# MLP up-projection of a hybrid decoder layer: product 2 of two tile pairs computed together by a second seven-product scheme

## The chip, the core and the metric

The kernel runs on one core of one Trainium2 chip. TensorE (PE) multiplies matrices, VectorE (DVE), ScalarE (ACT) and GpSimd (POOL) work elementwise, SyncE (SP) and the queues of ACT and POOL issue DMA transfers. Each engine takes its instructions in the order in which they were built; semaphores tie the engines together. The metric is the device time of one execution in microseconds.

## The reference

One layer of a decoder, fp32, for 1024 prompt tokens and 8 x 8 decode tokens: RMS norm, one input projection, two mixers (retention and sliding-window attention), output projection, residual; then the part that matters here:

```python
h = x + jnp.concatenate([o_r, o_s], axis=-1) @ w_out
hf = rms_norm(h, norm_ffn_gain)
h = h + jnp.square(jax.nn.relu(hf @ w_up)) @ w_down     # w_up (1024, 4096), w_down (4096, 1024)
```

All 1088 tokens (T) go through the layer as one batch.

## The kernel before

**Three passes for one product.** Every fp32 operand is split into a high part (a cast to the multiplier's type on ACT) and a low part (the difference, on DVE): `halve`, lines 792 and 793. `mm3` multiplies high by high, low by high and high by low into one PSUM bank (lines 176 to 178), so a 128x128 block times 272 columns is three matmuls.

**Seven products.** The up stage works on tile pairs `fp` = 0 to 15, 256 features each (two tiles of 128 rows). The 1024 inputs are two halves of 512, the 1088 tokens are two superchunks `s` of two quarters of Q = 272. So for each pair and superchunk there is a 2x2 by 2x2 block product, and it is made of seven products in place of eight (Strassen's scheme in Winograd's form): `PROD = (1, 2, 6, 5, 7, 4, 3)`. The right sides (`ops`: B11, B21, B22 and T1 to T4, split) are made once and stay in SBUF. The left sides come from `left`: a generator that loads the pair's four blocks a11, a12, a21, a22 as two raw tiles of 512 KB (`rawload`, issued on ACT's queue, line 807, three buffers with the tag "raw"), makes four sums on POOL (`comb`, line 1047: numbers 5, 6, 7 and 3) and splits each of the seven for PE (`wsplit`, tags wa and wb, four buffers each). A product of one superchunk is 4 x 3 = 12 matmuls.

**Results.** Banks x, y and z for each superchunk collect the products: 1, 6, 7 and 4 add up in x, and ACT copies x after 1, 6 and 7 (line 1142) because the running value is needed; before PE writes x again, that copy must be done. Product 2 goes into bank y, which DVE adds to the copy of product 1 (line 1121). DVE then scales (`act`, line 1126), ACT squares into `ra` (line 1127), POOL makes the four differences for the down stage's own seven products (`sub`, line 1175: four for each superchunk), and SP stores both to DRAM (`u_d`). `ra` and `rb` have one buffer, so ACT's squares of the next pair wait until POOL has read those of this one.

**The order.** The order of the products is written out in `up`; where the instructions of the engines land relative to each other is decided by the tile scheduler, which keeps each engine's queue as one fixed list. `issue_after` ties an instruction behind another. In the stretch of pairs 3 to 8 and on, `split_down` prepares pieces of w_down ahead (lines 1211 to 1216).

Of the kernel before, what the change touches and what calls it, by code (L numbers as in the profile page):

```python
# [36 lines left out]
def hymba_layer(ctx: ExitStack, tc: tile.TileContext, a: dict, o: dict):  # L37
# [753 lines left out]
    def halve(hi, lo, src, lo_eng):  # L791
        nc.scalar.copy(hi, src)  # L792
        lo_eng.tensor_tensor(lo, src, hi.bitcast(F32), ALU.subtract)  # L793
# [243 lines left out]
    def left(order, src, name, lo_eng, raw_tag="raw", raw_pool=None, s_tag="S", s_pool=None, tags=("wa", "wb"), raws=None, sums=None, stored=None):  # L1037

        r1, r2 = raws or (
            rawload(src[:, i * 1024 : i * 1024 + 1024], f"{name}_r{i + 1}", raw_tag, raw_pool) for i in range(2)  # L1040
        )
        a11, a12, a21, a22 = r1[:, :512], r1[:, 512:], r2[:, :512], r2[:, 512:]
        have = {1: a11, 2: a12, 4: a22, **(sums or {})}

        def comb(i, p_, q_, op):
            t_ = have[i] = (s_pool or mid).tile([P, 512], F32, tag=s_tag, name=f"{name}_s{i}", bufs=10 if s_tag == "Sb" else 4)
            nc.gpsimd.tensor_tensor(t_, p_, q_, op)
# [52 lines left out]
    um = ux.enter_context(pool("u", side="right"))  # L1100

    last_sub, last_store, last_sq = {}, [None], [None]

    def up(fp):
        gen = chain(ready, gen0) if fp == 0 else left(
            PROD, a["w_up"][fp], f"wu{fp}", nc.vector, tags=("wa", "wa", "wb", "wb"))
        x, y, z = ([bank(f"ps{n}{s}") for s in range(2)] for n in "xyz")
        home = {1: (x, True), 2: (y, True), 6: (x, False), 5: (z, True), 7: (x, False), 4: (x, False), 3: (z, False)}
        ra, rb = ([um.tile([P, n, Q], F32, tag=f"r{n}{s}", name=f"r{n}t{fp}_{s}") for s in range(2)] for n in (3, 4))
        held, wait, ws = {}, [], {}  # L1110
        order = [(i, s) for i in PROD for s in range(2)]
        if fp == 0:

            order = [(1, 0), (1, 1), (2, 0), (6, 0), (5, 0)] + [(i, 1) for i in (2, 6, 5)] + order[8:]

        def tq(n, s):
            return um.tile([P, Q], F32, tag="tq", name=f"{n}{fp}_{s}", bufs=9)

        def add(n, s, bank_):
            t_ = held[n, s]  # L1120
            nc.vector.tensor_tensor(t_, t_, bank_, ALU.add)
            return t_

        def act(t_, src, s, h, dst):

            nc.vector.scalar_tensor_tensor(t_, src, 0.0, rsf[:, s, h, :], ALU.max, ALU.mult)  # L1126
            return nc.scalar.activation(dst, t_, AF.Square)

        for i, s in order:
            if i not in ws:  # L1130
# [9 lines left out]
            if i in (1, 6, 7):  # L1140
                t_ = held[i, s] = tq(f"m{i}", s)
                nc.scalar.copy(t_, bk)  # L1142
# [22 lines left out]
            if i == 3:
                t_ = add(6, s, bk)
                if fp == 15 and s:
                    with tc.issue_after(squared.ins):
# [4 lines left out]
                t1, t2, t3, t4 = (rb[s][:, i_, :] for i_ in range(4))
                eng = nc.vector if fp in (0, 15) and s else nc.gpsimd
                sub = lambda o_, p_, q_: eng.tensor_tensor(o_, p_, q_, ALU.subtract)
# [32 lines left out]
    def split_down(f, c):  # L1208
# [222 lines left out]
```

## Time and profile before

| what | value |
|---|---|
| median of 3 runs | 1182.31 us (1181.42 to 1185.21) |
| profiled execution | 1183.0 us, span 1181.2 us |
| PE, DVE, ACT, POOL busy | 99%, 70%, 43%, 42% of the span |
| up stage, first to last psx matmul of op_0h | 496.0 to 835.1 us |
| granted clock | 0.999 |
| HBM read, written | 117.45 MB, 55.71 MB |

In a row of groups stand the line, the engine, the operation, output and inputs, shapes, count, busy time and mean of one in ns, and the idle time before them with what ended it. In a row of waits stand who waited for whom, the total, the count and the longest. In a row of windows stand the stretch, its length, and for PE, weight load, DVE, ACT and POOL the busy time with its count, then granted clock, DMA share and GB/s. In a row of the timeline stand start, duration, engine and instruction. Transfers have their size and the median time from issue to landing.

### The profile page before, as it was taken

The page shows a single profiled execution, that of the slowest core. Times are in us where ns is not written, and L with a number is a line of the kernel's source. Part 1 is how long each engine was busy: PE and PEld are TensorE (multiplying, and loading weights), DVE is VectorE, ACT ScalarE, POOL GpSimd, SP SyncE. Part 2 cuts the span into 40 slices and gives each one's busy share as a digit, 9 for nine tenths or more (in the row PEclk, how much of TensorE's full clock was granted, in tenths as well). Part 3 has the DMA queues.
Part 4 walks back from the last instruction along what each step waited for, and adds up shares of the span by engine and source line. Part 5 has one row for each costly group of instructions (what it writes and reads, how often), then busy time and mean ns, then how long its engine had stood idle before and what let it go on. Part 6 is the DMA issues. An engine that isn't in the chain of part 4 may idle for free.

```text
span 1181.2 us, 23556 instructions
## 1 busy us (share of the span) xinstructions
PE 1168.7 (99%) x9405; PEld 1124.5 (95%) x9405; DVE 831.6 (70%) x1551; ACT 512.5 (43%) x1060; POOL 492.7 (42%) x393
## 2 busy tenths in 40 slices
PE   8999999999999999999999999999999999999998
PEld 8999988989879899999999999999999999999998
DVE  7556868732258769888666667667678787888676
ACT  8343544553234447654444444444643423333231
POOL 0135334332255542457666766667374142053000
PEclk9999999999999999999999999999999999999999
DMA  7221334333625554343454445534795446443225
GB/s 248 73 62 63 96 104 163 104 118 90 192 67 175 180 169 160 126 136 143 149 176 141 166 157 171 170 123 151 235 383 179 149 163 203 150 157 98 77 59 189
DMA packets 106181, 174.69 MB, mean 148 GB/s; under 512 B 12319, under 2 KB 71647, under 8 KB 105815
## 3 DMA queue, kind: packets, MB, share of 16 engines
q1 hardware_dynamic: 92711, 129.04, 33.0%
q10 hardware_dynamic: 10800, 35.23, 9.2%
q0 software_dynamic: 2560, 8.91, 2.4%
q8 instruction: 74, 1.21, 0.4%
q14 instruction: 36, 0.29, 0.1%
HBM read 117.45 MB, written 55.71 MB: 147 GB/s over the span
## 4 chain that ended last, share of the span: by engine, by line
PE 83%; DVE 6%; DMA 5%; issue 3%; POOL 1%; ACT 1%; SPq 0%; DVEq 0%; POOLq 0%; ACTq 0%
PE psd L177 9%; PE psd L178 9%; PE psd L176 9%; PE psx L176 5%; PE psx L178 5%; PE psx L177 5%; PE psz L176 2%; PE psz L178 2%; PE psz L177 2%; PE pst L176 2%; PE pst L177 2%; PE pst L178 2%; PE psf L176 2%; PE psf L178 2%; PE psf L177 2%
## 5 line engine op out<-in xcount | busy, mean ns | idle before, releaser
L177 PE MATMUL psd<-uh,wd_w 128*128 128x272 f32 x896 | 259.2, 289 | 0.0
L178 PE MATMUL psd<-ul,wd_w 128*128 128x272 f32 x896 | 257.6, 288 | 0.3 <-DVE ul L793 0.3
L176 PE MATMUL psd<-uh,wd_w 128*128 128x272 f32 x896 | 257.8, 288 | 0.0
L176 PEld LDWEIGHTS psd<-uh,wd_w 128*128 128x128 f32 x896 | 169.1, 189 | 0.0
L178 PEld LDWEIGHTS psd<-ul,wd_w 128*128 128x128 f32 x896 | 168.5, 188 | 0.5 <-DVE ul L793 0.5
L177 PEld LDWEIGHTS psd<-uh,wd_w 128*128 128x128 f32 x896 | 168.4, 188 | 0.0
L1299 DVE TENSOR_TENSOR a<-a,psd 128x272 f32<-128x272 f32 x248 | 101.5, 430 | 50.7 <-PE psd L178 50.6
L793 DVE TENSOR_TENSOR wu_w<-wu_s,wu_w 128x512 fp32r<-128x512 f32 x64 | 58.4, 917 | 54.1 <-ACT wu_w L792 53.3
L792 ACT CAST wd_w<-wd_s 128x512 fp32r<-128x512 f32 x64 | 36.8, 617 | 113.2 <-PE psd L178 100.4
L793 DVE TENSOR_TENSOR ul<-ur,uh 128x1088 fp32r<-128x1088 f32 (+1 forms) x57 | 81.9, 1465 | 5.5 <-ACT uh L792 5.5
L176 PE MATMUL psx<-op_1h,wu_w 128*128 128x272 f32 x256 | 74.2, 290 | 0.3 <-ACT m L1142 0.3
L176 PE MATMUL psx<-op_0h,wu_w 128*128 128x272 f32 x256 | 74.1, 290 | 0.0
L178 PE MATMUL psx<-op_1l,wu_w 128*128 128x272 f32 x256 | 74.1, 289 | 0.0
L178 PE MATMUL psx<-op_0l,wu_w 128*128 128x272 f32 x256 | 74.1, 289 | 0.0
L177 PE MATMUL psx<-op_1h,wu_w 128*128 128x272 f32 x256 | 73.7, 288 | 0.0
L177 PE MATMUL psx<-op_0h,wu_w 128*128 128x272 f32 x256 | 73.7, 288 | 0.0
L1126 DVE SCALAR_TENSOR_TENSOR m<-m,rsf 128x272 f32<-128x272 f32 x96 | 71.3, 743 | 2.9 <-ACT rsf L915 0.5
L792 ACT CAST uh<-ur 128x1088 fp32r<-128x1088 f32 (+1 forms) x57 | 59.8, 1085 | 16.7 <-PE psd L177 9.1
L366 POOL TENSOR_TENSOR sp<-sp,ssp 128x1024 f32<-128x1024 f32 (+1 forms) x16 | 28.6, 1789 | 88.4 <-DVE ssp L365 60.0
L176 PE MATMUL psf<-hnh,wqk_hi 128*128 128x384 f32 (+1 forms) x192 | 63.5, 331 | 0.2 <-DVE qkst L518 0.2
L178 PE MATMUL psf<-hnl,wqk_hi 128*128 128x384 f32 (+1 forms) x192 | 63.1, 329 | 0.0
L177 PE MATMUL psf<-hnh,wqk_lo 128*128 128x384 f32 (+1 forms) x192 | 62.8, 327 | 0.0
(345 smaller groups left out, 3619.2 us busy)
## 6 DMA issues: line engine op xcount, KB each, us to landing
ur<-u_d SPq DMA_DIRECT2D x53, 544.0 KB, 5.0
u_d<-r4t SPq DMA_DIRECT2D x32, 544.0 KB, 3.2
wu_r<-in_w_up ACTq DMA_DIRECT2D x32, 512.0 KB, 4.5
wd_r<-in_w_down ACTq DMA_DIRECT2D x30, 512.0 KB, 6.8
u_d<-r3t SPq DMA_DIRECT2D x32, 408.0 KB, 2.7
y<-in_xY POOLq DMA_DIRECT2D x16, 272.0 KB, 3.5
y_d<-y POOLq DMA_DIRECT2D x16, 272.0 KB, 3.1
yt<-y_d SPq DMA_DIRECT2D x16, 272.0 KB, 2.8
```

The lines of the kernel that those rows point to most:

```text
L176: nc.tensor.matmul(ps, lh, rh, start=first, stop=False, skip_group_check=more)
L177: nc.tensor.matmul(ps, ll, rh, start=False, stop=False, skip_group_check=more)
L178: return nc.tensor.matmul(ps, lh, rl, start=False, stop=last, skip_group_check=more)
L366: nc.gpsimd.tensor_tensor(s, s, ss.unsqueeze(2).broadcast_to([P, 4, n]), ALU.mult)
L792: nc.scalar.copy(hi, src)
L793: lo_eng.tensor_tensor(lo, src, hi.bitcast(F32), ALU.subtract)
L1126: nc.vector.scalar_tensor_tensor(t_, src, 0.0, rsf[:, s, h, :], ALU.max, ALU.mult)
L1299: added[i] = nc.vector.tensor_tensor(to, to, ps, ALU.add).ins
```

## The change

For pairs 4 to 15 product 2, which is a12 times B21, leaves the pair. The product 2 of pairs `fp` and `fp + 1` over both superchunks is seen as one 2x2 by 2x2 product itself: two pairs by two quarters of 256 inputs on the left, two quarters by two superchunks on the right. It is made of seven small products of 2 x 3 = 6 matmuls each (`second`), run between the products of the pair ahead (`trail`: odd pairs 3 to 13), into banks ps2x, ps2y and ps2z. ACT copies four of the small results (line 1192) and DVE adds three (line 1195) into the tiles `tp2`; in its own pair, product 1 is then added to `tp2` (line 1253), scaled in place (1254) and squared (1266). Pairs 0 to 3 stay as they were. The right sides of the small products, three of them split sums of quarters of B21, are made once in pairs 2 and 3 (`prepare`). The left sides come from `left2`: one more raw load of 512 KB for two pairs (a12 of both, line 1153), four sums of 128x256 on POOL (1160 to 1167), three splits of 512 and one of 256. Of the `tq` buffers six are left of nine. Lines of the changed kernel move: copies of products are line 1257, comb stays 1047, differences are 1296, the sums with banks are 1229, scaling and squares 1234 and 1235.

```diff
@@ in left: comb
-            nc.gpsimd.tensor_tensor(t_, p_, q_, op)
+            last_comb[name, i] = nc.gpsimd.tensor_tensor(t_, p_, q_, op).ins
@@ new, ahead of up
+    L2 = 4
+    quarter = {(kh, s): [t_[:, 2 * kh : 2 * kh + 2, :] for t_ in ops[B21][s]] for kh in range(2) for s in range(2)}
+    tcomb = {i: [l2.tile([P, 2, Q], F32R, tag=f"x{i}{x}", name=f"x{i}{x}") for x in "hl"] for i in (2, 3, 4)}
+    tcomb[1] = quarter[0, 1]
+    RIGHT2 = {1: quarter[0, 0], 2: quarter[1, 0], 3: quarter[1, 1], 4: tcomb[4], 5: tcomb[1], 6: tcomb[2], 7: tcomb[3]}
...
+    def prepare():
...
+        for k in range(2):
...
+            e22 = join(nc.vector, last_stt[0], quarter[1, 1], k)
+            e21 = join(nc.gpsimd, behind, quarter[1, 0], k)
+            e11 = join(nc.gpsimd, behind, quarter[0, 0], k)
+            e12 = join(nc.vector, last_stt[0], quarter[0, 1], k, home)
+            nc.vector.tensor_tensor(e22, e22, e12, ALU.subtract)
+            nc.vector.tensor_tensor(e12, e12, e11, ALU.subtract)
+            nc.vector.tensor_tensor(e11, e22, e11, ALU.add)
+            nc.vector.tensor_tensor(e21, e21, e11, ALU.subtract)
...
+    def left2(fp, tags):
+        raw = mw.tile([P, 1024], F32, tag="raw", name=f"wp{fp}_r", bufs=3)
+        nc.scalar.dma_start(
+            raw.rearrange("p (f n) -> p f n", f=2), a["w_up"][fp : fp + 2, :, 512:1024].rearrange("f p n -> p f n")
+        )
+        a11, a12, a21, a22 = (raw[:, 256 * i : 256 * i + 256] for i in range(4))
+        yield wsplit(raw[:, :512], tags[0], f"wp{fp}_a", nc.vector)
...
+        nc.gpsimd.tensor_tensor(s1, a21, a22, ALU.add)
+        nc.gpsimd.tensor_tensor(s2, s1, a11, ALU.subtract)
+        nc.gpsimd.tensor_tensor(s3, a11, a21, ALU.subtract)
+        yield wsplit(s23, tags[1], f"wp{fp}_s23", nc.vector)
+        w = (mid if tags[2] == "wb" else mw).tile([P, 2, 512], F32R, tag=tags[2], name=f"wp{fp}_d", bufs=4)
+        halve(w[:, 0, :256], w[:, 1, :256], a22, nc.vector)
+        yield w
+        nc.gpsimd.tensor_tensor(s4, a12, s2, ALU.subtract)
+        yield wsplit(s14, tags[3], f"wp{fp}_s14", nc.vector)
+    def second(fp, tags):
...
+        copies = {1: (0, 0), 6: (0, 1), 7: (1, 1), 4: (1, 0)}
+        sums = {2: (0, 0), 5: (1, 1), 3: (0, 1)}
...
+            for k in range(2):
+                lh, ll = (got[n][:, j, c0 + k * 128 : c0 + k * 128 + 128] for j in range(2))
+                rh, rl = (v[:, k, :] for v in RIGHT2[i])
+                mm3(bk, lh, ll, rh, rl, first and k == 0, k == 1, not first)
...
@@ in up
+        trail = fp >= L2 - 1 and fp % 2 == 1 and fp < 15
+        prods = PROD if fp < L2 else (1, 6, 5, 7, 4, 3) if fp == 15 else (1, 5, 6, 7, 4, 3)
...
-        order = [(i, s) for i in PROD for s in range(2)]
+        order = [(i, s) for i in prods for s in range(2)]
+        if trail:
+            n = len(prods) - 5
+            for at, i in ((n, 1), (n, 2), (n + 1, 6), (n + 2, 7), (n + 3, 4), (n + 4, 5), (n + 5, 3)):
+                order.insert(2 * at + len(order) - 2 * len(prods), (i, 2))
...
+            if i == 1 and fp >= L2:
+                t_ = tp2[fp, s]
+                nc.vector.tensor_tensor(t_, t_, bk, ALU.add)
+                last_stt[0] = nc.vector.scalar_tensor_tensor(t_, t_, 0.0, rsf[:, s, 0, :], ALU.max, ALU.mult).ins
...
+            if fp >= L2 and (i, s) == (6 if trail else 7, 1):
+                for s_ in range(2):
+                    with tc.issue_after(last_copy[0]):
+                        nc.scalar.activation(ra[s_][:, B11, :], tp2[fp, s_], AF.Square)
```

Two places of the built order, on the engines that wait there. The first is POOL, from the sums for one pair to the differences of the pair before. In names, the number behind wu is the pair, s5, s6, s7 and s3 are comb's sums, wp10 belongs to the small products of pairs 10 and 11, r4t7 holds the differences of pair 7. Before:

```order
L1047 TENSOR_TENSOR wu9_s5_8355<-wu9_r2_8289 128x512
L1047 TENSOR_TENSOR wu9_s6_8357<-wu9_s5_8355,wu9_r1_8287 128x512
L1047 TENSOR_TENSOR wu9_s7_8417<-wu9_r1_8287,wu9_r2_8289 128x512
L1047 TENSOR_TENSOR wu9_s3_8491<-wu9_r1_8287,wu9_s6_8357 128x512
L1175 TENSOR_TENSOR r4t7_0_7753<-r127_0_7977,r3t7_0_7751 128x272
L1175 TENSOR_TENSOR r4t7_0_7753<-r3t7_0_7751,r127_0_7977 128x272
```

and now, behind wu9_s5, wu9_s6 and the first two sums of wp10 (one row each):

```order
L1161 TENSOR_TENSOR wp10_s2_8485<-wp10_s1_8486,wp10_r_8432 128x256
L1296 TENSOR_TENSOR r4t7_0_7853<-r127_0_8115,r3t7_0_7851 128x272
L1296 TENSOR_TENSOR r4t7_0_7853<-r3t7_0_7851,r127_0_8115 128x272
L1167 TENSOR_TENSOR wp10_s1_8486<-wp10_r_8432,wp10_s2_8485 128x256
L1296 TENSOR_TENSOR r4t7_0_7853<-r3t7_0_7851,r4t7_0_7853 128x272
L1296 TENSOR_TENSOR r4t7_1_7854<-r127_1_8136,r3t7_1_7852 128x272
L1296 TENSOR_TENSOR r4t7_1_7854<-r3t7_1_7852,r127_1_8136 128x272
L1296 TENSOR_TENSOR r4t7_0_7853<-r3t7_0_7851,r4t7_0_7853 128x272
L1047 TENSOR_TENSOR wu9_s7_8542<-wu9_r1_8397,wu9_r2_8399 128x512
L1296 TENSOR_TENSOR r4t7_1_7854<-r3t7_1_7852,r4t7_1_7854 128x272
L1047 TENSOR_TENSOR wu9_s3_8639<-wu9_r1_8397,wu9_s6_8456 128x512
```

The four sums of a pair stood together ahead of the eight differences; now the last two, which are the last readers of the raw tiles, stand behind the sums of wp10 and seven differences.

The second place is ACT at the same time: the copies of product 7 (m7 and the pair, m78 for pair 8) and what stands ahead of them. Before:

```order
L1127 ACTIVATE r3t7_0_7751<-m17_0_7774 128x272 [waits DMAHW1_49,DVE_49,Pool_49]
L1142 COPY m67_0_7842<-psx0_7745 128x272 [waits PE_49]
L807 DMA wu9_r2_8289<-in_w_up 128x1024 [waits DMAHW6_49,DVE_49]
L1127 ACTIVATE r3t7_1_7752<-m17_1_7788 128x272 [waits DMAHW2_49,Pool_49]
L1142 COPY m67_1_7856<-psx1_7746 128x272 [waits PE_49]
L792 CAST wu8_w5_8124<-wu8_s5_8089 128x512
L792 CAST wu8_w3_8227<-wu8_s3_8225 128x512 [waits PE_49]
L1142 COPY m77_0_7902<-psx0_7745 128x272 [waits PE_49]
```

and now:

```order
L1257 COPY m68_0_8245<-psx0_8156 128x272 [waits PE_49]
L1257 COPY m68_1_8259<-psx1_8157 128x272 [waits PE_49,Activation_49]
L792 CAST wu9_w6_8501<-wu9_s6_8456 128x512
L807 DMA wu10_r1_8706<-in_w_up 128x1024 [waits DMAHW1_49,Pool_49]
L1257 COPY m78_0_8278<-psx0_8156 128x272 [waits PE_49]
L1257 COPY m78_1_8295<-psx1_8157 128x272 [waits PE_49]
```

The issue of a raw load used to wait for DVE and for the load before it; now this one waits for POOL, and the copies of product 7 stand right behind it.

More of the change, by code (lines that the diff above doesn't have):

```diff
@@ L1102, in hymba_layer @@
     last_sub, last_store, last_sq = {}, [None], [None]
-    def up(fp):
-        gen = chain(ready, gen0) if fp == 0 else left(
-            PROD, a["w_up"][fp], f"wu{fp}", nc.vector, tags=("wa", "wa", "wb", "wb"))
-        x, y, z = ([bank(f"ps{n}{s}") for s in range(2)] for n in "xyz")
+    L2 = 4
+    l2 = opx.enter_context(pool("l2", side="left"))
+    quarter = {(kh, s): [t_[:, 2 * kh : 2 * kh + 2, :] for t_ in ops[B21][s]] for kh in range(2) for s in range(2)}
+    tcomb = {i: [l2.tile([P, 2, Q], F32R, tag=f"x{i}{x}", name=f"x{i}{x}") for x in "hl"] for i in (2, 3, 4)}
@@ new lines, in second, with product @@
+    def second(fp, tags):
+        weights, banks, got = left2(fp, tags), {}, []
+        use = {1: (0, 0, "x"), 2: (0, 256, "y"), 6: (1, 0, "x"), 7: (1, 256, "x"), 4: (2, 0, "x"), 5: (3, 0, "z"), 3: (3, 256, "z")}
+        copies = {1: (0, 0), 6: (0, 1), 7: (1, 1), 4: (1, 0)}
+        sums = {2: (0, 0), 5: (1, 1), 3: (0, 1)}
+        def product(i):
+            n, c0, name = use[i]
+            if n == len(got):
+                got.append(next(weights))
+            first = name not in banks
+            if first:
+                banks[name] = bank(f"ps2{name}")
+            bk = banks[name]
+            for k in range(2):
+                lh, ll = (got[n][:, j, c0 + k * 128 : c0 + k * 128 + 128] for j in range(2))
+                rh, rl = (v[:, k, :] for v in RIGHT2[i])
+                mm3(bk, lh, ll, rh, rl, first and k == 0, k == 1, not first)
+            f_, s = copies[i] if i in copies else sums[i]
+            if i in copies:
+                t_ = tp2[fp + f_, s] = um.tile([P, Q], F32, tag="t2", name=f"t2{fp + f_}_{s}", bufs=4)
+                nc.scalar.copy(t_, bk)
+            else:
+                t_ = tp2[fp + f_, s]
+                nc.vector.tensor_tensor(t_, t_, bk, ALU.add)
+        return product
@@ new lines, in up @@
+    def up(fp):
+        trail = fp >= L2 - 1 and fp % 2 == 1 and fp < 15
+        prods = PROD if fp < L2 else (1, 6, 5, 7, 4, 3) if fp == 15 else (1, 5, 6, 7, 4, 3)
+        tags, tags2 = ("wa", "wb"), ("wb", "wb", "wa", "wa")
+        if fp < L2 - 1:
+            tags = ("wa", "wa", "wb", "wb")
+        elif trail and fp < L2:
+            tags, tags2 = ("wa", "wb", "wb", "wb", "wa", "wa", "wa"), ("wa", "wa", "wb", "wb")
+        elif trail:
+            tags = ("wa", "wa", "wa", "wb", "wb", "wb")
+        gen = chain(ready, gen0) if fp == 0 else left(prods, a["w_up"][fp], f"wu{fp}", nc.vector, tags=tags)
+        two = second(fp + 1, tags2) if trail else None
+        x, y, z = ([bank(f"ps{n}{s}") if n != "y" or fp < L2 else None for s in range(2)] for n in "xyz")
@@ L1124, in act @@
         def act(t_, src, s, h, dst):
-            nc.vector.scalar_tensor_tensor(t_, src, 0.0, rsf[:, s, h, :], ALU.max, ALU.mult)
+            last_stt[0] = nc.vector.scalar_tensor_tensor(t_, src, 0.0, rsf[:, s, h, :], ALU.max, ALU.mult).ins
             return nc.scalar.activation(dst, t_, AF.Square)
         for i, s in order:
+            if s == 2:
+                two(i)
+                continue
             if i not in ws:
@@ L1147, in up @@
                     act(*wait.pop())
+            if fp >= L2 and (i, s) == (6 if trail else 7, 1):
+                for s_ in range(2):
+                    with tc.issue_after(last_copy[0]):
+                        nc.scalar.activation(ra[s_][:, B11, :], tp2[fp, s_], AF.Square)
+            if fp == 2 and (i, s) in ((2, 1), (6, 0), (6, 1), (5, 0), (7, 1), (4, 0), (4, 1), (3, 1)) or (fp, i, s) == (3, 2, 1):
+                next(ready2)
             if fp == 0 and (i, s) == (5, 0):
```

39 lines of the change are left out of this document (33 added, 6 removed).

## The prediction

> **What bounds the kernel now.** I read the page's busy shares and chain first, then PE's waits, then windows over the up stage.
>
> ```profile
> span 1181.2 us, 23556 instructions
> PE 1168.7 (99%) x9405; PEld 1124.5 (95%) x9405; DVE 831.6 (70%) x1551; ACT 512.5 (43%) x1060; POOL 492.7 (42%) x393
> PE psz L177 <- DVE wu_w L793: 0.7, 1, 0.7
> PE psx L176 <- ACT m L1142: 0.3, 1, 0.3
> L176 PE MATMUL psx<-op_0h,wu_w x256: 283/289/373, 496.0 to 835.1; 128*128 128x272 f32 x128
> 560.00:820.00 260.00, 260.00 (x2064) 260.00 (x2063) 175.36 (x268) 115.28 (x267) 168.02 (x148) 1.00 0.47 159
> ```
>
> TensorE sets the time. In the up stage (from 496.0 to past 835 us) PE waits twice, 1.0 us in all. In the 260 us of the sixth row it never waits: a matmul of 272 columns every 260/2064 = 0.126 us at granted clock 1.00. Beside it DVE is busy for 67%, ACT for 44%, POOL for 65%. So a matmul taken away there is worth 0.126 us, as long as the other engines still keep ahead. Whether they do is the question.
>
> ```profile
> POOL r4t L1175 <- ACT r L1127: 53.1, 16, 4.9
> POOL wu_s L1047 <- DMA wu_r<-in_w_up: 48.2, 13, 4.9
> ACT r3t L1127 <- POOL r4t L1175: 32.7, 28, 3.0
> ```
>
> POOL idles twice in a tile pair of 21.2 us, 3.3 and 3.7 us a time (53.1/16, 48.2/13). And ACT, whose copies free the PSUM banks, already waits for POOL 28 times, 1.2 us each; today PE's slack hides it.
>
> **What is removed.** For pairs 4 to 15, product 2 took 24 matmuls of a pair; two pairs now share 7 x 2 x 3 = 42 in place of 48. Six times 6 gone: 36 x 0.126 = **4.5 us**. The built order has exactly 36 PE rows fewer. The banks, weights and results keep their sizes, so nothing else on PE shrinks.
>
> **What is added, per two pairs.** POOL: four 128x256 sums. DVE: one 128x512 and one 128x256 subtraction and three 272-wide sums more (the four additions of product 1 replace those of product 2). ACT: one cast and one half cast. One more load of 512 KB, issued from ACT. By sums alone there is room: DVE gains under 3 us in 41.6, POOL 4 at most of the 14 that it idles. The load adds 8% to the 6.6 MB that two pairs move at 159 GB/s and a DMA share of 0.47. What hides the small products' four copies on ACT (0.38 each, as many as product 1's were) is the 12 and more matmuls, 1.5 us, laid between two products of one bank; without that cover each would cost its 0.38. The smaller scratch area and the six in place of nine tq buffers issue nothing. So the averages do not decide it; the queues do.
>
> **The queues.** Three raw buffers serve all weight loads (rawload). Before, two pairs needed four loads, now five, and a load waits until the last reader of its buffer is done. That reader is often POOL's product-3 sum (L1047), which the scheduler now puts behind most of the difference instructions (L1296); and ACT, which issues the loads in order, has the two copies of product 7 (L1257) queued behind the load. PE needs these copies to go on with product 4. Both orders are in the section on the change. The prices:
>
> ```profile
> L1126 DVE SCALAR_TENSOR_TENSOR m<-m,rsf 128x272 f32<-128x272 f32 x96 | 71.3, 743 | 2.9 <-ACT rsf L915 0.5
> L793 DVE TENSOR_TENSOR wu_w<-wu_s,wu_w 128x512 fp32r<-128x512 f32 x64 | 58.4, 917 | 54.1 <-ACT wu_w L792 53.3
> L793 DVE TENSOR_TENSOR wu_w<-wu_r,wu_w 128x512 fp32r<-128x512 f32 x48 | 47.0, 982 | 6.9 <-ACT wu_w L792 5.7 <-DMA ur<-u_d 0.2
> L1121 DVE TENSOR_TENSOR m<-m,psz 128x272 f32<-128x272 f32 x64 | 27.9, 435 | 23.1 <-ACT m L1142 14.8 <-PE psz L178 8.3
> L1215 DVE TENSOR_TENSOR pw<-pw 128x256 fp32r<-128x256 f32 x8 | 3.4, 419 | 0.0
> L1142 ACT COPY m<-psx 128x272 f32<-128x272 f32 x96 | 36.0, 378 | 30.4 <-PE psx L178 29.6 <-PE psn L911 0.4 <-issue 0.2
> L1127 ACT ACTIVATE r3t<-m 128x272 f32<-128x272 f32 x64 | 27.6, 432 | 67.8 <-DVE m L1126 32.7 <-POOL r4t L1175 32.7 <-issue 2.4
> L1175 POOL TENSOR_TENSOR r4t<-r3t,r4t 128x272 f32<-128x272 f32 x60 | 62.0, 1042 | 1.3
> L1175 POOL TENSOR_TENSOR r4t<-r,r3t 128x272 f32<-128x272 f32 x30 | 30.1, 1004 | 53.1 <-ACT r L1127 53.1
> L1175 POOL TENSOR_TENSOR r4t<-r3t,r 128x272 f32<-128x272 f32 x30 | 29.5, 985 | 0.0
> L1047 POOL TENSOR_TENSOR wu_s<-wu_r,wu_r 128x512 f32<-128x512 f32 x16 | 25.9, 1622 | 0.0
> L1047 POOL TENSOR_TENSOR wu_s<-wu_r,wu_s 128x512 f32<-128x512 f32 x16 | 23.8, 1486 | 3.1 <-DVE wu_w L793 3.1
> L1047 POOL TENSOR_TENSOR wu_s<-wu_r 128x512 f32<-128x512 f32 x15 | 21.2, 1410 | 52.2 <-DMA wu_r<-in_w_up 48.2 <-DVE wu_w L793 4.0
> L1047 POOL TENSOR_TENSOR wu_s<-wu_s,wu_r 128x512 f32<-128x512 f32 x15 | 21.1, 1408 | 1.2
> wu_r<-in_w_up ACTq DMA_DIRECT2D x32, 512.0 KB, 4.5
> ```
>
> DVE's and POOL's means hide a spread, seen in single instructions (DVE, DVE, DVE, DVE, then POOL):
>
> ```profile
> 577.84 0.46 DVE L1126 SCALAR_TENSOR_TENSOR m<-m,rsf 128x272 f32<-128x272 f32 x1
> 579.40 0.69 DVE L793 TENSOR_TENSOR wu_w<-wu_s,wu_w 128x512 fp32r<-128x512 f32 x1
> 580.01 1.53 DVE L1126 SCALAR_TENSOR_TENSOR m<-m,rsf 128x272 f32<-128x272 f32 x1
> 586.97 1.26 DVE L793 TENSOR_TENSOR wu_w<-wu_s,wu_w 128x512 fp32r<-128x512 f32 x1
> 579.41 1.84 POOL L1047 TENSOR_TENSOR wu_s<-wu_r,wu_r 128x512 f32<-128x512 f32 x1
> 585.98 0.77 POOL L1175 TENSOR_TENSOR r4t<-r,r3t 128x272 f32<-128x272 f32 x1 [3.27 <-ACT r L1127]
> 588.82 1.22 POOL L1175 TENSOR_TENSOR r4t<-r,r3t 128x272 f32<-128x272 f32 x1
> 598.28 1.29 POOL L1047 TENSOR_TENSOR wu_s<-wu_r 128x512 f32<-128x512 f32 x1 [4.47 <-DMA wu_r<-in_w_up]
> ```
>
> The DVE instruction of 580.01 takes 1.53 us in place of 0.46 and ends at 581.54, 0.3 us behind the POOL instruction that ran from 579.41 to 581.25. Where both engines work out of SBUF, each waits for the other's instruction to end; DVE's PSUM readers (0.435) do not wait. So POOL's 272-wide instruction costs 0.77 to 1.22, the 512-wide one 1.29 to 1.84.
>
> *Loop A* runs from ACT's copy of product 7 in an odd pair (7, say) to that copy in the next even pair (8). (1) The copy, 0.38. (2) Six DVE instructions up to the subtraction that frees the raw buffer for the new load: two sums 0.44, two scalings 0.74, subtractions 0.92 and 0.98, together 4.3; POOL works beside them, so the means hold. (3) The load, 4.5. (4) Thirteen POOL instructions up to the product-3 sum of pair 9: seven differences at their mean of 1.01, 7.1; the product-7 and product-3 sums 1.62 + 1.49 = 3.1; four of 128x256, which no row shows. Those lie between 0.72 (0.77 by width, unhindered) and 1.01; I take 0.77, as part of them run beside an idle DVE: 3.1. Together 13.3. (5) ACT then issues the load for pair 10 and copies, 0.38. Sum 22.9 us. In the meantime PE has from product 4 of pair 7 to product 4 of pair 8: 168 matmuls, 21.2 us. PE waits **1.7 us**.
>
> *Loop B* runs from there to the copy of product 7 in pair 9. Copy 0.38; eight DVE instructions up to the half split that frees the buffer, with POOL idle meanwhile (its next instruction waits for this load), so at the short rows: 3 x 0.44 + 3 x 0.46 + 0.69 + 0.42 = 3.8; load 4.5; twelve POOL instructions, eight differences and four sums, until ACT's squares may overwrite what POOL reads. Unhindered 8 x 0.77 + 4 x 1.29 = 11.3, at the means 8 x 1.01 + 5.9 = 14.0; DVE has little to do there, so the middle, 12.6. Square and copy 0.8. Sum 22.1 against 162 matmuls, 20.4: PE waits **1.7 us**.
>
> Each loop closes on itself, since the next starts at the late copy: the time is lost each time round. Five of each (A into pairs 6 to 14, B into 5 to 13): 5 x 3.4 = **17 us**. Bounds: with every instruction unhindered A is 19.3 us and B 20.8, so nothing or 0.4 us is lost; with B's POOL at its means and a 256-wide sum at 1.01, A loses 2.6 and B 3.1, 28 us in all.
>
> **The quartered operands** are made in pairs 2 and 3: 20 DVE instructions of 272, four on POOL, eight casts. DVE's room there:
>
> ```profile
> 530.00:550.00 20.00, 19.67 (x156) 19.45 (x155) 18.12 (x27) 9.19 (x22) 14.56 (x12) 1.00 0.44 145
> 550.00:570.00 20.00, 20.00 (x161) 20.00 (x160) 14.28 (x21) 9.01 (x21) 14.32 (x14) 1.00 0.42 151
> ```
>
> DVE is free for 1.9 and 5.7 us in these 40. The 20 cost 8.8 us unhindered (0.44 each) and 15 hindered (0.74), so they overrun by 1 to 7 us; how much of that PE sees depends on how far ahead the weights stand, which no row tells. I take 1.5 us, between 0 and 4.
>
> **Sum.** -4.5 + 17 + 1.5 = +14.0 on the profiled execution of 1183.0 us (span 1181.2 and 1.8 around it); it lies 0.7 above the median of the runs, 1182.3. I take **1196 us**, 1.2% slower.
>
> **Rivals.** (1) *POOL's idle time absorbs it.* For: of 41.6 us POOL idles 14 and gains 4 at most; unhindered rows close loop A in 19.3 of 21.2 us. Against: one idle stretch is the wait for a load, and loads are now what is late. It decides if POOL's thirteen take under 11.6 us. Then 1182.3 - 4.5 = 1178, faster. (2) *The loops are late by half a microsecond to one*, as if POOL ran at 12 us in both: 1 us a pair and the operands' 1.5 eat the gain, 1183. (3) *POOL and DVE hinder each other throughout.* Taking each instruction out of SBUF at its short row, two pairs before need 16 x 0.77 + 8 x 1.29 = 22.6 on POOL and 14 x 0.69 + 12 x 0.46 = 15.2 on DVE, together 37.8 of 42.3 us; after the change 25.5 + 16.3 = 41.8 of 41.6. If the two can only take turns, nothing is left over, and every delay stays: both loops at their upper bounds, 28 us, and 4 for the operands, 1182.3 - 4.5 + 32 = 1210. Against: the short rows overlap a little at their ends (579.40 + 0.69 is past 580.01), and one of the two often has nothing to do.
>
> The Trainium skill, "SBUF — State Buffer", section "SBUF: two separate sides", states rival 3's ground as a rule: DVE and GpSimd share a port pair under an exclusive lock, held for the whole instruction, and the other fully blocks. The trace agrees as far as the instruction of 580.01 goes, 1.53 us in place of 0.46. The rule speaks against adding work for both engines at once; by it alone the pairs would be full, by the rows' overlap not quite.
>
> That the change does not do what it says is ruled out by the 36 PE rows.
>
> **Chances.** The forecast (1187 to 1204) 0.70; rival 1 0.10; rival 2 (1179 to 1187) 0.09; rival 3 (beyond 1204) 0.11. The range for 8 in 10 is 1182 to 1206. A measurement of this kernel tells about 0.3%, 3.5 us, from no change: faster 0.09 (rival 1, less its part above 1178.8), same 0.06 (that part and most of rival 2), slower 0.85.
>
> **What would show it.** In the waits of the changed kernel: PE psx waiting for ACT m (L1257) or for what follows it, some ten times, 1 to 2.5 us each, at intervals that alternate near 23 and 22 us; on ACT a wait for POOL wu_s or a pause ahead of the load at L807, right in front of L1257; POOL waiting for the load wp_r. Wrong, if PE waits under 0.3 us a pair from pair 5 on (rival 1), if POOL's product-3 sum ends before PE has reached product 7, or if the waits sit elsewhere: at the products of the small scheme (ps2x, ps2z), or at weights whose DVE subtraction comes late, which would make DVE the cause.

## The result, and the profile after

The changed kernel takes **1202.4 us** (median of six runs, 1200.8 to 1204.5) against 1182.8 before (1181.4 to 1185.2): **1.65% slower**, ratio 1.0165 with a 95% interval of 1.0148 to 1.0182. The forecast was 1196, slower; the time lies inside its range.

The page of the changed kernel, its span and the row of busy times, and then the window over the same 260 us that the prediction began with (columns: stretch, length, busy time and instructions of PE, of PE's weight loads, DVE, ACT, POOL; granted clock, DMA share, GB/s):

```profile
span 1202.5 us, 23639 instructions
PE 1171.7 (97%) x9369; PEld 1121.7 (93%) x9369; DVE 846.0 (70%) x1601; ACT 518.2 (43%) x1080; POOL 508.9 (42%) x421
```

```profile
560.00:820.00 260.00, 244.33 (x1890) 240.26 (x1890) 171.15 (x287) 111.31 (x266) 171.37 (x159) 0.99 0.44 154
```

PE has the 36 matmuls fewer (9369), but in 260 us it starts 1890 in place of 2064. DVE is a little less busy in that window than before (171.2 us, 175.4 then) and POOL a little more (171.4, 168.0 then): as a sum they were not overrun, they and PE waited for one another.

The up stage, from the start of the first to the start of the last matmul into psx, psy, psz or ps2, grew from 343.9 to 362.2 us. The rest of the 21.3 us between the two spans isn't the change: the stage begins at 496.0 us before and at 498.2 after, and in the ten further executions below, whose code up to there is the same, anywhere from 495.6 to 501.1. What comes behind it took 341.3 and 342.1 us. So the length of the stage, taken from the one profiled execution of each kernel, is the finer measure, and it stands beside each time below.

The waits of the changed kernel (us in total, times, longest), PE's own first:

```profile
PE psx L176 <- ACT m L1257: 8.4, 9, 2.5
PE ps2x L176 <- ACT t L1192: 7.2, 6, 1.6
PE psx L176 <- DVE t L1253: 1.6, 1, 1.6
POOL wu_s L1047 <- DMA wu_r<-in_w_up: 51.0, 8, 9.3
ACT m L1257 <- POOL wu_s L1047: 29.5, 5, 7.1
POOL wp_s L1160 <- DMA wp_r<-in_w_up: 22.3, 4, 6.3
```

The fifth row isn't there before the change: ACT's copy of product 7 waits for POOL's product-3 sum, which it doesn't read. Between the two stands the issue of a load. The timeline shows one round, loop A first, in pair 6 (columns: start, us, engine, line, operation, tiles; in brackets the idle time before it and what ended it; POOL twice, ACT three times, PE):

```profile
640.07 0.80 POOL L1160 TENSOR_TENSOR wp_s<-wp_r 128x256 f32<-128x256 f32 x1 [5.71 <-DMA wp_r<-in_w_up]
...
652.15 1.27 POOL L1047 TENSOR_TENSOR wu_s<-wu_r,wu_s 128x512 f32<-128x512 f32 x1
646.67 0.39 ACT L1257 COPY m<-psx 128x272 f32<-128x272 f32 x1 [1.18 <-PE psx L178]
...
653.46 0.34 ACTq L807 DMA_DIRECT2D wu_r<-in_w_up  x1
653.84 0.67 ACT L1257 COPY m<-psx 128x272 f32<-128x272 f32 x2 [6.26 <-POOL wu_s L1047]
654.27 0.39 PE L176 MATMUL psx<-op_0h,wu_w 128*128 128x272 f32 x1 [1.65 <-ACT m L1257]
```

The load of the small products' weights lands, POOL works through thirteen instructions until 653.4, the raw buffer is free, ACT issues the next load at 653.46 and only then comes to the copies that PE has waited for. Loop B follows, in pair 7 (the issue of its load on ACT, POOL twice, ACT four times, with PE between them by time):

```profile
657.79 0.33 ACTq L807 DMA_DIRECT2D wu_r<-in_w_up  x1
...
663.19 1.29 POOL L1047 TENSOR_TENSOR wu_s<-wu_r 128x512 f32<-128x512 f32 x1 [9.05 <-DMA wu_r<-in_w_up]
...
671.95 1.29 POOL L1047 TENSOR_TENSOR wu_s<-wu_r,wu_s 128x512 f32<-128x512 f32 x1
673.27 0.33 ACTq L807 DMA_DIRECT2D wu_r<-in_w_up  x1
...
674.63 0.39 ACT L1192 COPY t<-ps2x 128x272 f32<-128x272 f32 x1
675.07 0.39 PE L176 MATMUL ps2x<-x4h,wp_d 128*128 128x272 f32 x1 [1.27 <-ACT t L1192]
675.90 0.43 ACT L1266 ACTIVATE r3t<-t 128x272 f32<-128x272 f32 x1 [0.88 <-POOL r4t L1296]
676.24 0.65 ACT L1257 COPY m<-psx 128x272 f32<-128x272 f32 x2
```

Here ACT is held twice: by the load that waits for the product-3 sum (673.27), with the copy of a small product behind it, and by the square that waits for POOL's differences (675.90), with the copies of product 7 behind it. PE loses 1.43 us at ps2x and 0.36 at psx.

The whole bill of the stage, from the distances between the starts of successive matmuls over their usual 0.126 us: four A waits (pairs 6, 8, 10, 12) of 1.81, 1.76, 1.77 and 2.69, 8.0 us; four B waits (pairs 5, 7, 9, 11), 1.02 + 0.36, 1.43 + 0.36, 1.57 + 0.35 and 1.72 + 0.34, 7.2 us; 0.28, 0.82 and 1.62 in pairs 2 and 3, 2.7 us; 0.38 and 1.78 in the last round, pairs 13 and 14, 2.2 us; 1.5 us of slowed clock (the last section). With the gain, -4.5, that is 17.1 of the 18.3. Behind each of some twenty waits the second matmul starts 0.23 us after the first in place of 0.126, about 2.0 us more, and three waits of about 0.2 add 0.7. Against this some 1.5 us are saved, because waits of 0.86 and 0.49 that the stage had before the change are gone.

Two of these waits differ from the rest. The fourth A wait goes with a load that took 5.35 us from its issue (772.62) to POOL's start (777.97), where the first two took 4.2. And the 1.78 us in pair 14 are no link of the loops: PE waits there for DVE's sum out of psx (L1253, the third row of the waits), and DVE had worked without a pause since 822.48, with four instructions out of SBUF at 1.00 to 1.35 us beside POOL's, where the prediction's short rows have 0.46 and 0.69.

### The profile page after: what moved, and what is told of

Its sections match the earlier page's. It is cut to its first block, busy times and chain, and to the rows that moved or that the text cites. A ratio compares the mean times of both kernels' runs of the same rounds, so it can differ in the third digit from the quotient of the medians.

```text
span 1202.5 us, 23639 instructions
## 1 busy us (share of the span) xinstructions
PE 1171.7 (97%) x9369; PEld 1121.7 (93%) x9369; DVE 846.0 (70%) x1601; ACT 518.2 (43%) x1080; POOL 508.9 (42%) x421
## 4 chain that ended last, share of the span: by engine, by line
PE 30%; POOL 9%; DMA 5%; DVE 4%; issue 3%; ACT 1%; ACTq 0%; POOLq 0%; DVEq 0%
PE psd L177 9%; PE psd L178 9%; PE psd L176 9%; POOL r4t L1296 5%; POOL wu_s L1047 3%; DMA wu_r<-in_w_up 2%; DMA wp_r<-in_w_up 1%; DMA ur<-u_d 1%; DVE wu_w L793 1%; DVE m L1234 1%; PE psx L176 1%; PE psx L178 1%; PE psx L177 1%; DVE m L1229 1%; POOL wp_s L1161 0%
## 5 line engine op out<-in xcount | busy, mean ns | idle before, releaser
L176 PEld LDWEIGHTS psx<-op_0h,wu_w 128*128 128x128 f32 x256 | 48.4, 189 | 13.1 <-ACT m L1257 11.2
```

Of the source, the lines that this page charges most:

```text
L176: nc.tensor.matmul(ps, lh, rh, start=first, stop=False, skip_group_check=more)
```

## The experiments

Where a run leaves out part of the computation, its expectation says so. The table gives the up stage in us, the median time in us, and its ratio to runs of the kernel before that were taken beside it, with the 95% interval.

| run | up stage | time | ratio | edit to the changed kernel |
|---|---|---|---|---|
| before | 343.9 | 1182.8 | | |
| the change | 362.2 | 1202.4 | 1.0165 (1.0148 to 1.0182) | |
| e1 | 350.9 | 1190.6 | 1.0061 (1.0037 to 1.0085) | ACT's order: squares behind the copies |
| e2 | 351.5 | 1192.2 | 1.0075 (1.0051 to 1.0098) | POOL's order: sums ahead of the differences |
| e3 | 353.2 | 1195.2 | 1.0095 (1.0077 to 1.0114) | raw loads issued by SP |
| e4 | 339.3 | 1181.6 | 0.9977 (0.9967 to 0.9986) | POOL's four sums left out |
| e5 | 358.2 | 1200.3 | 1.0145 (1.0129 to 1.0160) | the four sums on DVE |
| e6 | 351.4 | 1190.4 | 1.0061 (1.0046 to 1.0075) | the four sums made, not read |
| e7 | 340.8 | 1180.1 | 0.9972 (0.9963 to 0.9981) | e1, e2, two differences on DVE, last operand later |
| e8 | 340.8 | 1180.7 | 0.9979 (0.9970 to 0.9988) | e1, e2, e5, last operand later |
| e9 | 342.1 | 1181.5 | 0.9987 (0.9977 to 0.9997) | e1 and e2 |
| e10 | 353.8 | 1192.8 | 1.0083 (1.0065 to 1.0101) | two differences on DVE alone |

### e1: the squares behind the copies

```diff
-            if fp >= L2 and (i, s) == (6 if trail else 7, 1):
+            if fp >= L2 and (i, s) == (7, 1):
```

> In odd pairs ACT's two squares of product 1 (L1266) stand behind the copies of product 7 instead of behind those of product 6. Nothing is taken away; one link of loop B is cut (copy of product 7 behind squares that wait for POOL's differences). Theory 1, a ring: loops A and B are two halves of one ring around two pairs, 22.9 + 22.1 = 45.0 us against 41.6 of matmuls, and a copy that isn't late in the odd pair gives the even pair its slack back (between the end of product 7 and the start of product 4 lie 18 matmuls, 2.3 us). Then both waits go: 5 x (1.8 + 1.9) = 18.5 us less, 1184 us, and PE psx waits for ACT m or ACT t under 0.3 us a pair from pair 5 on. Theory 2, each loop for itself: B's waits go (9.5 us), A's 1.8 stay at product 4 of the even pairs: 1193 us. Theory 3, POOL and DVE hinder each other and are full: no work left either, so 1200 to 1203 us, the waits come out elsewhere.

Measured: 350.9 us, 1190.6. The number is nearer to theory 2's, the places are not: the waits of the *even* pairs (A), which the edit doesn't touch, are gone up to pair 12 (1.0 us in pair 14 is the wait for DVE again), and those of the *odd* pairs (B) stay, four times, 1.7 to 2.25 us, now at psx. So a copy that is less late in one pair does give slack to the next, as theory 1 had it; but B has a second branch that was left. (The scheduler answered the edit on PE as well: in odd pairs 12 matmuls of the next pair's product 1 now stand ahead of product 4, and the small product 4 behind it. That is why the wait shows at psx and no longer at ps2x; about as many matmuls lie ahead of product 4 as before.) One round of it in time order, from the timeline of e1 (ACT, POOL, ACT, ACT, DVE, ACT's queue, POOL, POOL, ACT's queue, ACT):

```profile
682.54 0.43 ACT L1235 ACTIVATE r<-m 128x272 f32<-128x272 f32 x1 [1.19 <-DVE m L1234]
683.05 0.83 POOL L1296 TENSOR_TENSOR r4t<-r,r3t 128x272 f32<-128x272 f32 x1 [5.35 <-ACT r L1235]
...
692.40 0.62 ACT L792 CAST wp_s<-wp_s 128x512 fp32r<-128x512 f32 x1 [3.69 <-POOL wp_s L1161]
692.92 0.67 ACT L1257 COPY m<-psx 128x272 f32<-128x272 f32 x2
698.79 0.42 DVE L793 TENSOR_TENSOR wp_d<-wp_r,wp_d 128x256 fp32r<-128x256 f32 x1
699.25 0.33 ACTq L807 DMA_DIRECT2D wu_r<-in_w_up  x1
705.09 1.47 POOL L1047 TENSOR_TENSOR wu_s<-wu_r 128x512 f32<-128x512 f32 x1 [7.95 <-DMA wu_r<-in_w_up]
713.59 1.26 POOL L1047 TENSOR_TENSOR wu_s<-wu_r,wu_s 128x512 f32<-128x512 f32 x1
714.88 0.33 ACTq L807 DMA_DIRECT2D wu_r<-in_w_up  x1
715.79 0.67 ACT L1257 COPY m<-psx 128x272 f32<-128x272 f32 x2
```

In the even pair POOL makes seven differences and three sums one behind the other from 683.05; ACT's cast of such a sum is held until 692.40 and the copies of product 7 stand behind it; DVE's work on them frees the raw buffer at 699.2; the load lands 5.8 us later; POOL has nine instructions up to and with the product-3 sum, which ends at 714.85; the next load is issued, and the copies of the odd pair start at 715.79. The waits repeat every 43.8 us, with 41.6 of matmuls in between. POOL's idle 8 us ahead of 705.09 is no reserve: it is the load, and the load waited for work that waited for POOL.

### e2: the sums ahead of the differences

```diff
                 comb(6, have[5], a11, ALU.subtract)
-            if i == 7:
+                if s_tag == "S" and order != PROD:
+                    comb(7, a11, a21, ALU.subtract)
+                    comb(3, a12, have[6], ALU.subtract)
+            if i == 7 and 7 not in have:
                 comb(7, a11, a21, ALU.subtract)
-            if i == 3:
+            if i == 3 and 3 not in have:
                 comb(3, a12, have[6], ALU.subtract)
```

> POOL makes the sums of products 7 and 3 (L1047) of a pair right behind those of 5 and 6, ahead of the differences of the pair before (L1296), not between and behind them. Same instructions, another order: the raw buffers come free some 7 us (seven differences of 1.01) earlier, the differences end 3.1 us later. Theory 1, a ring: loop A falls from 22.9 to about 15.8 us and the ring from 45.0 to 38; if the later differences hold nothing, both waits go: 1184 us. Theory 2, each loop for itself: A's 1.8 us at product 4 of the even pairs go, B stays with its two sums moved but as many POOL instructions ahead of the squares: 1193 us. Theory 3, port full: 1200 to 1203 us. My own doubt: with the sums ahead, POOL and DVE work side by side where DVE was alone, so new waits of some tenths at product 6 are to be looked for.

Measured: 351.5 us, 1192.2. The number is theory 2's, but by luck: A's waits and B's at ps2x, the branch of the product-3 sum, are gone, 0.36 us stays at psx in each odd pair, B's other branch, and the rest is new. The waits of e2:

```profile
PE psx L176 <- DVE t L1256: 5.3, 9, 1.7
PE psx L176 <- ACT m L1260: 1.3, 6, 0.3
```

The first row is the new wait that was looked for: at product 6 of the even pairs, 0.7 and 0.5 us each time (1.8 in pair 14), for DVE, whose sum out of psx stands behind a subtraction that took 1.26 us, where the prediction's short row had 0.69. DVE's timeline of e2 there:

```profile
685.13 1.26 DVE L793 TENSOR_TENSOR wp_a<-wp_r,wp_a 128x512 fp32r<-128x512 f32 x1
686.32 0.42 DVE L1256 TENSOR_TENSOR t<-t,psx 128x272 f32<-128x272 f32 x1
```

The waits still repeat every 43.5 us against 41.6 of matmuls: PE is held at other places, and a round of two pairs still takes longer than PE's own work in it.

### e3: the raw loads on SP's queue

```diff
-        nc.scalar.dma_start(raw, src)
+        (nc.sync if name[:3] in SPQ else nc.scalar).dma_start(raw, src)
```

SPQ holds beginnings of names that take in the weights of pairs 4 to 15, and those of pair 1 too: 26 of the 32 loads leave ACT's queue.

> The loads of the raw weights of pairs 4 to 15 (L807) are issued from SP's queue in place of ACT's; the load of the small products' weights (L1153) stays on ACT. This takes the load that waits for a raw buffer out from ahead of ACT's copies of product 7 in the even pairs. Theory 1, a ring: the copy no longer waits for the product-3 sum, so A's waits go, and B with them if the ring closed only through that copy: 1184 us; but if B runs through POOL's differences and ACT's squares by itself, B's 1.9 us a time stay: 1193 us, which is what theory 2 says in any case. Theory 3, port full: 1200 to 1203 us. If SP holds the loads back behind its stores, which wait for POOL's differences, weights come late: then PE waits for psx with DVE or ACT work on wu_w ahead, and the time stays near 1200.

Measured: 353.2 us, 1195.2. Even pairs: no wait left but one of 1.34 us in pair 14, for DVE. Odd pairs: 0.43, 2.18, 0.99, 2.64 and 0.66 us, at ps2x. ACT's timeline in pair 7 of e3 shows the branch that e1 had cut:

```profile
668.96 0.43 ACT L1268 ACTIVATE r3t<-t 128x272 f32<-128x272 f32 x1 [4.62 <-POOL r4t L1298]
669.42 0.39 ACT L1194 COPY t<-ps2x 128x272 f32<-128x272 f32 x1
669.71 0.43 ACT L1268 ACTIVATE r3t<-t 128x272 f32<-128x272 f32 x1
670.04 0.66 ACT L1259 COPY m<-psx 128x272 f32<-128x272 f32 x2
```

No load stands ahead of the copies, but a square that is held for 4.6 us by POOL's differences does. e1 and e3 are each other's complement: B runs over the square *and* over the load, and each kept it up where the other was cut.

### e4: POOL's four sums left out, and e6: made but not read

```diff
-        nc.gpsimd.tensor_tensor(s1, a21, a22, ALU.add)
-        nc.gpsimd.tensor_tensor(s2, s1, a11, ALU.subtract)
-        nc.gpsimd.tensor_tensor(s3, a11, a21, ALU.subtract)
-        yield wsplit(s23, tags[1], f"wp{fp}_s23", nc.vector)
+        yield wsplit(raw[:, 512:], tags[1], f"wp{fp}_s23", nc.vector)
...
-        nc.gpsimd.tensor_tensor(s4, a12, s2, ALU.subtract)
-        yield wsplit(s14, tags[3], f"wp{fp}_s14", nc.vector)
+        yield wsplit(raw[:, 256:768], tags[3], f"wp{fp}_s14", nc.vector)
```

e6 has the two lines with wsplit alone.

> Leaves out POOL's four 128x256 sums per two pairs (L1160 to L1167): the small products take raw blocks as weights, so they are not the seven products of the scheme, with all other instructions as they were. POOL has 3.1 us less to do per two pairs (four at 0.77), the ring comes to 45.0 - 3.1 = 41.9 against 41.6. Theory 1, a ring: hardly 0.3 us per two pairs left, 1184 to 1187 us. Theory 2, each loop for itself: A falls to 19.8 and its 1.8 us go, B's 1.9 stay: 1193 us. Theory 3, port full (41.8 of 41.6 us by the short rows): 3.1 us less to do in the port per two pairs gives at most 6 x 3.1 back, 1184 too, so this run only tells theory 2 from the others.

> POOL makes the four sums as in the change, but nothing reads them: the small products take raw blocks as weights (so the computation is not the scheme's), as in the run without the sums. POOL's queue is as long as in the change; only ACT's cast of a sum (which stands ahead of the copies of product 7 of the odd pair and waits for POOL) and DVE's subtraction no longer wait for it. Theory 1a, the ring runs through ACT's cast: 339 to 342 us of up stage, 1180 to 1184. Theory 1b, it runs through POOL's queue to the product-3 sum and the load: as in the change, 360 us, 1200. Both by turns: between, 350 us, 1190. Theory 3, port full: as in the change, 1200 to 1203.

Measured: e4 339.3 us, e6 351.4. Without the sums the stage is 4.6 us shorter than before, the full price of the 36 matmuls, 36 x 0.126 = 4.5, and no wait of the loops is left. (The time of e4, 1181.6 against 1183.2 beside it, shows only 1.6 of it; its runs spread from 1178.8 to 1187.1, and its profiled execution came to the stage only at 501.1 us.) With the sums made and not read, about half of the loss stays: 1.48, 2.64, 1.49 and 1.50 us in pairs 6 to 12, where the copy of psx that PE waits for (at 691.80 in pair 8) follows a load that ACT issues only at 691.43, behind POOL's sum. So the sums act by both ways: somebody waits for them, and they lengthen POOL's queue. Whether the first is ACT's cast, in front of the copies, or DVE's subtraction, e6 doesn't separate. "Both by turns" was the guess that held.

### e5: the four sums on DVE

```diff
-        nc.gpsimd.tensor_tensor(s1, a21, a22, ALU.add)
+        nc.vector.tensor_tensor(s1, a21, a22, ALU.add)
```

and so for all four.

> The four 128x256 sums per two pairs (L1160 to L1167) are made on DVE in place of POOL; nothing else. Theory 1, the ring runs through POOL's queue: POOL is relieved exactly as in the run without the sums (up stage 339.3 us there, 362.2 with them), so PE's waits for ACT m and ACT t go; DVE gets four times 0.42 to 0.8, 1.7 to 3.2 us of 41.6, and if it has that much room the stage takes 340 to 343 us, the kernel 1181 to 1184. Theory 3, the port that both use is full: in place of 0.77 each the sums take 0.42 of it, 1.4 us per two pairs less, six times: 8 us less, 354 us, 1194. Theory 4, what counts is that somebody waits for these sums in order, whichever engine makes them: then DVE takes POOL's place in the ring, the waits stand at psx behind DVE t (L1253), and the stage stays near 360 us, the kernel near 1200.

Measured: 358.2 us, 1200.3: next to nothing won, theory 4. Most of the waiting in e5 is for DVE now:

```profile
PE psx L176 <- DVE t L1253: 5.4, 4, 1.7
PE psx L177 <- DVE wu_w L793: 5.1, 2, 2.6
```

And DVE's timeline shows one place where its room was of no use:

```profile
682.78 0.42 DVE L1160 TENSOR_TENSOR wp_s<-wp_r 128x256 f32<-128x256 f32 x1 [1.74 <-DMA wp_r<-in_w_up]
683.12 0.43 DVE L1229 TENSOR_TENSOR m<-m,psz 128x272 f32<-128x272 f32 x1
```

DVE stands still for 1.74 us in front of the first sum, because the load of the small weights hasn't landed, while a sum out of psz stands next in its queue. From there it has no pause up to the subtraction of 688.18, for which PE waits 2.55 us. A short instruction (0.42 here) was moved, and with it the wait for a load.

### e9: order alone, and e10: amount alone

e9 is e1 and e2 together: the same instructions on the same engines as in the change, in another order on ACT, POOL and (as in e1, by the scheduler) on PE. e10 keeps the order and takes two differences per two pairs from POOL:

```diff
-                sub(t3, b22, r12)
+                (nc.vector.tensor_tensor(t3, b22, r12, ALU.subtract) if fp >= 4 and fp % 2 == 0 else sub(t3, b22, r12))
```

> Order alone, no work moved between engines, the computation complete: e1 and e2 together (squares of product 1 behind the copies of product 7 in odd pairs; sums of products 7 and 3 ahead of the differences). Theory A, it is the order in which ACT and POOL take their work that closes the ring: then the two cuts together do what e7 did, 341 to 343 us of up stage, 1180 to 1183. Theory B, it is POOL's amount (two differences of 1.0 us fewer per two pairs were what e7 had beside these cuts): then about 2 us per two pairs come back, five to six times, 350 to 353 us, 1190 to 1192, no better than either cut alone.

> The amount alone, order as in the change: one of the four differences of each superchunk in the even pairs from 4 on (t3) on DVE in place of POOL, two of 1.0 us per two pairs. Theory A, the order closes the ring: the ring loses 3.7 us per two pairs, POOL gives back 2.0 at most of it and DVE takes some tenths, five times: 354 to 357 us of up stage, 1194 to 1197. Theory B, the amount: the waits go, as in e7, 341 to 345 us, 1180 to 1185. Theory 3, port full: 0.66 us per two pairs back, 358 us, 1198.

Measured: e9 342.1 us and 1181.5, theory A; e10 353.8 us and 1192.8. e9's row of busy times and its window over the middle of the stage:

```profile
PE 1164.4 (99%) x9369; PEld 1118.4 (95%) x9369; DVE 852.4 (72%) x1601; ACT 516.7 (44%) x1080; POOL 505.8 (43%) x421
```

```profile
590.00:800.00 210.00, 210.00 (x1668) 209.90 (x1667) 149.08 (x242) 92.90 (x224) 148.52 (x142) 1.00 0.49 170
```

1601, 1080 and 421 instructions on DVE, ACT and POOL, as in the change; PE runs through. Behind this window one wait is left, 0.95 us in pair 14, for DVE's sum out of psx. Before the change the same window held 1668 matmuls too; in the change it held 1521 (before, then the change):

```profile
590.00:800.00 210.00, 210.00 (x1668) 210.00 (x1667) 141.70 (x216) 93.47 (x218) 135.07 (x120) 1.00 0.47 159
590.00:800.00 210.00, 196.67 (x1521) 193.45 (x1520) 132.13 (x229) 87.54 (x209) 135.11 (x128) 0.99 0.46 159
```

147 x 0.126 = 18.5 us, all of it the order in which the queues take the same work. Less work in the old order (e10) wins back 8.4 of the 18.3 us.

### e7 and e8: toward a better version

Both have e1 and e2, and the split of the last quartered operand one product later in pair 3; e7 adds e10's edit, e8 adds e5's.

```diff
-            if ... or (fp, i, s) == (3, 2, 1):
+            if ... or (fp, i, s) == (3, 6, 1):
                 next(ready2)
```

> Toward a better version, the computation complete. Three links of the ring relieved at once: the sums of products 7 and 3 ahead of the differences (as e2), the squares of product 1 behind the copies of product 7 (as e1), and one of the four differences of each superchunk in even pairs (t3) on DVE in place of POOL, 2 x 1.0 us per two pairs off POOL and 0.9 to 1.5 on DVE; the cast and split of the last operand (product 5) one product later in pair 3. Theory 1, the ring: each alone left 350.9 and 351.5 us of up stage; together POOL is 2 to 9 us earlier at each link, no wait remains from pair 5 on, and the stage takes 343.9 - 4.5 and 1 to 3 us for pairs 2 to 4: 340.5 to 342.5, the kernel 1180 to 1182, not to be told from before (1183.2). Theory 3, port full: the port gains only 2 x 0.33 us per two pairs, 4 us in all: 1186 to 1198.

> The same with the other relief for POOL, the computation complete: the sums of products 7 and 3 ahead of the differences, the squares behind the copies of product 7, the last operand later, and the small products' four sums on DVE (as e5) in place of the two differences. Theory 1, the ring: 340.5 to 343 us of up stage, 1180 to 1183. If DVE's queue has become the tight one (theory 4), waits stand at psx behind DVE t: 345 to 350 us, 1185 to 1190. Theory 3, port full: 8 us less than the change, 1194.

Measured: both 340.8 us, 1180.1 and 1180.7, faster than before by 0.28% (0.19 to 0.37) and 0.21% (0.12 to 0.30). They are level with each other and the fastest complete kernels of the study, 22 us faster than the change. PE has no wait over 0.2 us between 590 and 830 us in either. e5's edit, worthless alone, does no harm once the order leaves slack.

## Why the prediction was right and wrong

- **PE bounds, a matmul is worth 0.126 us, the gain is 4.5.** Right: e4 shows 4.6 us in the stage.
- **Loop A, 1.7 us.** Right, term by term: from the copies in pair 5 (630.77) six DVE instructions from 631.17 to 635.86, 4.7 us (4.3 predicted), 4.2 from the issue of the load to POOL's start (4.5), thirteen POOL instructions from 640.07 to 653.42, 13.35 us (13.3); four A waits, the first three 1.76 to 1.81. The route was the one named: product-3 sum, load in front of the copies in ACT's queue. Cutting it at ACT (e3) ended the even pairs' waits.
- **Loop B, 1.7 us.** The size is right: twelve POOL instructions from 663.19 to 675.87, 12.7 us (12.6), and the load took 5.4 us from its issue at 657.79 to POOL's start, in place of 4.5; PE loses 1.4 to 2.1. The place is not: "until ACT's squares may overwrite what POOL reads" is only B's second branch. The first is the same load issue as in A, with the copy of a small product (L1192) behind it, so PE waits first at ps2x, a place that the prediction had listed under wrong. e1 and e3 show both branches.
- **"Each loop closes on itself, five of each, 17 us."** That they feed themselves is right; that they do so separately is not. They are halves of one ring: the A waits repeat at 45.4 and 45.6 us (654.3, 699.7, 745.3), the sum of the two predicted loops (45.0), against 41.6 of matmuls, and cutting a link of B (e1) ended A's waits. There were four full rounds, 15.2 us, and in the last round 2.2 in other places, 17.4 together. That this is so near to 17 is in part luck: a round cost 3.8 in place of 3.4, there was one fewer, and most of the last 2.2 us is the wait for DVE in pair 14, which the prediction didn't have.
- **Operands, 1.5 us by an overrun of DVE.** 2.7 us, inside the bounds of 0 to 4, but the mechanism fell. e9, where no loop is left, has the same 0.33, 0.82 and 1.62 us, and its timeline of ACT at the last of them reads:

```profile
581.71 0.43 ACT L1238 ACTIVATE r3t<-m 128x272 f32<-128x272 f32 x1 [4.60 <-POOL r4t L1299]
582.04 0.60 ACT L792 CAST wu_w<-wu_s 128x512 fp32r<-128x512 f32 x1
582.55 0.38 ACT L1195 COPY t<-ps2x 128x272 f32<-128x272 f32 x1
```

  Again a square that POOL holds back stands ahead of a small product's copy. DVE stood idle for 1.70 us up to 582.75, so it wasn't the engine that was late; POOL had worked without a pause since 569.07. In front of the copy behind the 0.82 stands a load, issued at 572.24, just when a DVE subtraction had ended (572.21), and before that subtraction DVE had idled for 1.31 us. e7 and e8, with the last operand's split later, have 0.97 us there. Why POOL's differences are that late in pair 3 was not tried by itself.
- **The sum, +14.0.** Measured +18.3 in the stage and 19.6 between the medians. The step that was too small is the list of terms, not the loops, which with their last round came out 0.4 above their term. The operands were 1.2 above theirs; the slowed clock (1.5), the start behind each wait (about 2.0) and the small waits (0.7) were not in the sum, and neither were the 1.5 us of waits from before the change, which it saved.
- **Rival 1, POOL's idle time absorbs it.** False for this order, true for another: in e9 the same POOL work fits with no wait between 590 and 800 us. The argument "one idle stretch is the wait for a load, and loads are now what is late" was the right one against it.
- **Rival 2, loops late by half a microsecond to one.** False: A lost 1.8 and B 1.4 to 2.1 us a time.
- **Rival 3, POOL and DVE full at their shared port.** Ruled out as the cause of the loss by e9: by the short rows the work was put at 41.8 of 41.6 us, and the same instructions fit. It still costs PE something in places: the wait in pair 14 and e2's waits at product 6 stand behind DVE instructions that ran long beside POOL's. The Trainium skill's rule ("SBUF — State Buffer", section "SBUF: two separate sides") that the one engine fully blocks the other still agrees with single rows, such as the 1.26 us subtraction in e2; as a sum over two pairs it did not bound the time here.

## What to carry to other kernels

When an added load or sum leaves every engine with idle time, write down for each in-order queue what stands *behind* each instruction that waits: here a load that waited for a buffer and a square that waited for a buffer each stood in front of copies that PE needed, and reordering at two places, with no work removed, was worth 20 us. Where such a wait closes into a ring, look for its parallel branches before cutting: one cut moved the wait to another place and won a little over half (e1 350.9, e2 351.5 of 362.2 us), two cuts won nearly everything (e9 342.1, and 340.8 in e7 and e8). Moving a short instruction to an engine with room also moves what it waits for, to the head of another queue.

## What the runs showed of the hardware that was not expected

TensorE's clock can fall after a short wait. Windows of the changed kernel around the 2.69 us wait in pair 12 (the figure behind the last bracketed busy time is the granted clock):

```profile
790.00:792.50 2.50, 0.43 (x3) 0.43 (x4) 0.44 (x1) 0.87 (x3) 1.94 (x3) 1.00 0.13 43
792.50:794.00 1.50, 1.50 (x10) 1.50 (x9) 1.44 (x4) 1.16 (x4) 0.00 (x0) 0.58 0.90 238
794.00:796.00 2.00, 2.00 (x11) 2.00 (x11) 1.87 (x5) 0.93 (x4) 0.00 (x0) 0.50 0.88 321
796.00:798.00 2.00, 2.00 (x17) 2.00 (x17) 0.88 (x2) 1.35 (x3) 0.00 (x0) 0.96 0.89 191
```

From 0.7 us behind the wait on, for 3.4 us, the granted clock is 0.50 and matmuls start every 0.227 us in place of 0.126: 1.5 us more for that one wait. In the up stages it happened twice in e3 (behind 2.18 and 2.64 us, 1.5 each), once in e5 (2.71, 1.2) and once in e6 (2.64, 1.1); in these last two the clock fell while PE still waited. It did not happen behind another 2.67 in e5 nor behind e1's 2.17, 2.25 and 2.09. Outside the up stage shorter waits had it too: in e4 two matmuls of the down stage that start 1.93 us apart, the second at 871.66, have this window behind them:

```profile
872.25:875.60 3.35, 3.35 (x17) 3.35 (x16) 3.35 (x8) 2.08 (x2) 0.50 (x1) 0.50 1.02 405
```

So a wait of 1.8 to 2.7 us cost another 1.1 to 1.5 us at some places and nothing at others, and its length alone doesn't decide. The Trainium skill ("TensorE: Matmul & The Clock Gate", section "Part 1: The HAM clock gate (the "warmup" mystery)") puts the drop after an idle window of about 3.4 us that runs freely. The half clock and the 3.4 us that it lasts agree; here less than 3.4 us of waiting was enough, and whether the place of the window decides, no run here shows.
